# Scheduling priority for the product evacuations of the first FFN group, with 4 raw and 7 operand buffers

## The chip, the cores and the metric

The kernel runs on one core of a Trainium2 chip. The metric is the device time of one execution in microseconds (us). A core has a matrix engine (PE in the profile; PEld is its weight load), a vector engine (DVE), a scalar engine (ACT), a GpSimd engine (POOL) and a queue engine (SP) that only issues transfers. Each works through its own list of instructions strictly in order; semaphores tie the lists together.

## The reference, cut to what matters

One decoder layer is applied to a prompt of 16 + 2048 tokens and to a sample group of 8 x 4 tokens, with the same weights: a mixer (three kinds of heads side by side, then an output product with `w_out`), and a SwiGLU FFN. The change touches the seam between the two and the FFN.

```
y = concat([ya, yb, yc]) @ w_out                 # (tokens, 1024) x (1024, 1024)
h = h + y
g, u = split(rmsnorm(h, norm_ffn) @ w_ffn_in)    # 1024 -> 2 x 2816
h = h + (silu(g) * u) @ w_ffn_out                # 2816 -> 1024
return rmsnorm(h, norm_final), states
```

All inputs are fp32. The kernel keeps fp32 quality by splitting each operand into a high and a low fp16 part and adding three products: high x high, high x low, low x high.

## The kernel before, in words

The kernel is one function, `trunk`, written in the Tile framework. The programmer writes operations and takes tiles from pools with a fixed number of buffers; a scheduler then fixes the order of each engine's list when the kernel is built. It takes the operation of best priority among those that are ready in its model; without further notice priority is the order of the text, and an operation that needs a buffer has to come behind the last reader of that buffer's previous content. Operations that are written under `tc.high_priority()` go ahead of the others that are ready.

**The seam.** After the mixer, `out_early` (L1071) walks over the pairs of 128-token tiles. For each tile it loads the mixer's output from HBM (`xT<-yT_scratch`, L978, SP), multiplies it by `w_out` on PE (48 matmuls of 512 columns for each tile, all at L212, product `wo`), adds the residual on DVE (L998) and stores `h`. The tile of the sample group and the 16 meta tokens (`y`, `xn`, L978 to L992) goes second to last. For the first pairs it also norms the rows and forms the FFN's moving operand (`prep`), stored on ACT's queue as `x_scratch<-pT` (L1043). `load_x2` (L1059) brings that operand of one group back with twelve transposing transfers `x<-x_scratch` (L1057, `DMA_TRANSPOSE`, SP). `interleave` (L874) writes several generators out in turn, one step of each at a time: first `outs`, which is `out_early`, is written out to its end, then `load_x2` of the first group.

**The FFN.** Tokens are worked in three groups of tiles: tiles 1 to 6, 7 to 12, and the rest with the short tile. Within a group the 11 pairs of hidden blocks come in four parts of 2, 3, 3 and 3, and each part is `hidden` for each of its pairs, then `down` for the part. Products of 2 x 2 blocks are made by a seven-product (Winograd) scheme. `quad` (L1230) makes one such product: 7 times 12 matmuls into a PSUM bank `s` (L1239), whose evacuation spreads over ACT, DVE and POOL (L1244 to L1252; POOL has two additions, L1248 and L1249). `hidden` (L1255) makes two quads, one for the gate and one for the up projection, with SiLU on ACT (L1259), the multiplication on DVE (L1262) and the seven operands of the next product as `hh`, high on ACT (L1268) and low on DVE (L1269). `down` (L1285) multiplies `hh` by the weights of `w_ffn_out` (L1292, product `dn`) and adds into the residual `xr` (L1302 to L1330).

**Weight preparation.** Only the first group prepares weights. `gu_operands` (L1179) and `dn_operands` (L1192) load an fp32 block `raw` (SP, L1186 and L1198) and form one operand tile `w`: four additions `sums` on POOL (`left`, L1015 to L1018, for the gate and up weights; `right`, L1022 to L1025, for the down weights), three high parts on ACT (L155) and three low parts on DVE (L156). There are four such tiles for each pair of hidden blocks from the gate and up weights, and two from the down weights, 66 in all. `kept` (L1128) stores each tile to HBM for the later groups, which load it again. The eight loads of the first four `raw` blocks, for the first pair of hidden blocks, are written ahead of the out products (`gu_first`). `raw` has 6 buffers and `w` has 6.

## Time and profile before

| what | value |
|---|---|
| time, median of 3 runs | 2420.63 us (2420.12 to 2420.94) |
| the profiled execution's own time | 2414.44 us |
| its span in the profile | 2412.7 us |
| PE busy | 2220.3 us (92%) |
| DVE busy | 1679.2 us (70%) |
| POOL busy | 1211.7 us (50%) |
| ACT busy | 943.5 us (39%) |
| mean granted clock of TensorE | 0.97 |

The shares are means over stages that differ. By the first matmul of `quad` the mixer and the out products take 1055 us, the first FFN group runs from there to 1602 us, the second from 1602 to about 2015 us with its last `down` running on beside it, and the third to the end. The profiled execution is 6.2 us shorter than the median of the timed runs, so a difference in the profile is to be added to the median, not the profile's end.

### The profile page before, as it was taken

How to read it: one execution, taken by the hardware profiler on the slowest of the kernel's cores; microseconds unless marked ns; L12 is line 12 of the kernel's file. 1: busy time of each engine (PE TensorE's matmuls, PEld its weight loads, DVE VectorE, ACT ScalarE, POOL GpSimd, SP SyncE). 2: the span in 40 equal slices, each digit the busy share in tenths (PEclk: the TensorE clock that was granted, in tenths of full speed). 3: DMA queues.
4: the chain of work that ended last, by engine and by line, in shares of the span. 5: the costliest groups of instructions: out<-in, count | busy, mean ns of one | idle time of the engine just before them, and what ended most of it. 6: DMA issues, size and time to landing. Idle time of an engine off the chain costs nothing. (4 is left out here: it accounts for less than half of the span.)

```text
span 2412.7 us, 51978 instructions
## 1 busy us (share of the span) xinstructions
PE 2220.3 (92%) x20298; PEld 1607.4 (67%) x20298; DVE 1679.2 (70%) x4030; ACT 943.5 (39%) x2526; POOL 1211.7 (50%) x1629
## 2 busy tenths in 40 slices
PE   6989999999999899896989979889999999999996
PEld 6677767767776445444657556567686767888886
DVE  8788988988988756558879677746454535655546
ACT  7554455554554432334343434422212123332323
POOL 7344344444443464549778788744232324544435
PEclk9999999999999899997999989899999999999998
DMA  7232333333223755996436545684324247744441
GB/s 258 50 63 69 66 67 68 75 61 74 66 64 73 173 183 192 275 330 222 153 139 231 196 158 191 191 287 185 148 108 168 108 152 199 269 176 175 177 174 38
DMA packets 294329, 364.95 MB, mean 151 GB/s; under 512 B 203808, under 2 KB 234480, under 8 KB 294067
## 3 DMA queue, kind: packets, MB, share of 16 engines
q1 hardware_dynamic: 285090, 331.02, 43.6%
q0 software_dynamic: 4384, 15.93, 1.7%
q10 hardware_dynamic: 4608, 14.68, 1.7%
q8 instruction: 159, 2.61, 0.4%
q14 instruction: 88, 0.71, 0.1%
HBM read 212.24 MB, written 103.50 MB: 131 GB/s over the span
## 5 line engine op out<-in xcount | busy, mean ns | idle before, releaser
L1239 PE MATMUL s<-x,w 128*128 128x384 f16 (+1 forms) x5544 | 826.4, 312 | 14.8 <-DMA w<-wgu_scratch 6.2
L1239 PEld LDWEIGHTS <-w 128*128 128x128 f16 x5544 | 542.6, 98 | 296.5 <-issue 13.8
L1292 PE MATMUL dn<-w,hh 128*128 128x256 f16 (+1 forms) x4158 | 444.4, 278 | 56.0 <-ACT hh L1268 23.6
L1292 PEld LDWEIGHTS <-hh 128*128 128x128 f16 (+1 forms) x4158 | 379.6, 99 | 119.8 <-ACT hh L1268 27.8
L212 PEld LDWEIGHTS <-xT 128*128 128x128 f16 (+1 forms) x1992 | 177.4, 99 | 191.4 <-issue 25.2
L1268 ACT ACTIVATE hh<-tmp 128x384 f16<-128x384 f32 (+1 forms) x231 | 112.4, 494 | 280.4 <-DVE tmp L1262 164.5
L1248 POOL TENSOR_TENSOR tmp<-tmp,tmp 128x384 f32<-128x384 f32 (+1 forms) x66 | 65.3, 990 | 279.0 <-ACT tmp L1247 271.8
L1269 DVE TENSOR_TENSOR hh<-tmp,hh 128x384 f16<-128x384 f32 (+1 forms) x231 | 144.5, 633 | 74.2 <-ACT hh L1268 72.5
L212 PE MATMUL wo<-wo,xT 128*128 128x512 f16 x768 | 180.8, 394 | 9.5 <-DVE xn L992 4.6
L156 DVE SCALAR_TENSOR_TENSOR w<-raw,w 128x512 f16<-128x512 f32 (+1 forms) x136 | 111.9, 855 | 7.0 <-ACT w L155 6.9
L1250 DVE TENSOR_TENSOR tmp<-s,tmp 128x384 f32<-128x384 f32 (+1 forms) x66 | 34.2, 518 | 107.3 <-PE s L1239 107.3
L212 PE MATMUL d<-xT,qf 128*128 128x128 f16 (+1 forms) x1632 | 107.7, 220 | 0.0
L156 DVE SCALAR_TENSOR_TENSOR w<-sums,w 128x1024 f16<-128x1024 f32 x68 | 96.9, 1427 | 11.4 <-ACT w L155 11.4
L1259 ACT ACTIVATE tmp<-tmp 128x384 f32<-128x384 f32 (+1 forms) x132 | 61.6, 489 | 107.9 <-DVE tmp L1250 52.6
L212 PE MATMUL d<-xT,bqk 128*128 128x128 f16 (+1 forms) x1632 | 100.6, 221 | 3.2 <-DVE e L278 3.2
L1324 DVE SCALAR_TENSOR_TENSOR xr<-dn,xr 128x256 f32<-128x256 f32 x192 | 78.7, 417 | 34.4 <-PE dn L1292 30.2
L212 PEld LDWEIGHTS <-qf 128*128 128x128 f16 x1632 | 94.4, 100 | 9.1 <-issue 4.1
L212 PEld LDWEIGHTS <-bqk 128*128 128x128 f16 x1632 | 94.0, 100 | 5.4 <-issue 4.5
L212 PE MATMUL d<-xT,cq 128*128 128x128 f16 (+1 forms) x1632 | 96.2, 217 | 0.0
L212 PE MATMUL d<-bvo,xT 128*128 128x512 f16 (+1 forms) x408 | 96.2, 380 | 0.0
L1262 DVE SCALAR_TENSOR_TENSOR tmp<-tmp,tmp 128x384 f32<-128x384 f32 (+1 forms) x132 | 71.9, 558 | 34.1 <-POOL tmp L1249 32.6
L212 PE MATMUL d<-aig,xT 128*128 128x512 f16 (+1 forms) x408 | 92.4, 379 | 3.4 <-DVE g L358 3.4
(536 smaller groups left out, 4064.6 us busy)
## 6 DMA issues: line engine op xcount, KB each, us to landing
w<-wgu_scratch SPq DMA_DIRECT2D x88, 896.0 KB
wgu_scratch<-w SPq DMA_DIRECT2D x44, 896.0 KB
w<-wdn_scratch SPq DMA_DIRECT2D x44, 896.0 KB
raw<-in_w_ffn_in_dram SPq DMA_DIRECT2D x88, 256.0 KB
wdn_scratch<-w SPq DMA_DIRECT2D x22, 896.0 KB
xs<-in_x_prompt_dram SPq DMA_DIRECT2D x26, 512.0 KB
x_scratch<-pT ACTq DMA_DIRECT2D x28, 448.0 KB
raw<-in_w_ffn_out_dram SPq DMA_DIRECT2D x22, 512.0 KB
```

What stands on the lines that cost most here:

```text
L156: V.scalar_tensor_tensor(lo, src, scale, hi, op0=ALU.mult, op1=ALU.subtract)
L212: T.matmul(out, lh(k, a), rh(k, b), start=(n == 0), stop=(n == 3 * nk - 1))
L1239: T.matmul(out, A[k // 2][p][:, a, k % 2 * P : k % 2 * P + P], x2[r][:, k // 2, op, k % 2, :n], start=i == 0, stop=i == 11)
L1248: G.tensor_tensor(r12, r12, r22, op=ALU.add)
L1250: V.tensor_tensor(r11, prod(A12, B21), r11, op=ALU.add)
L1259: S.activation(d, d, AF.Silu, scale=UF)
L1262: V.scalar_tensor_tensor(d, v, UF * HS, d, op0=ALU.mult, op1=ALU.mult)
L1268: S.activation(hi, v, AF.Copy)
L1269: V.tensor_tensor(lo, v, hi, op=ALU.subtract)
L1292: T.matmul(out, hh[p][:, q, a, off : off + L], ws[q][r][:, b], start=(q, p, r) == order[0], stop=(q, p, r) == order[-1])
L1324: V.scalar_tensor_tensor(x[:L, cc], m, UD, x[:L, cc], op0=ALU.mult, op1=ALU.add)
```

## The change

Three things change. Every vector, scalar and GpSimd instruction of `quad`, `hidden` and `down` is written under `tc.high_priority()`, through a small wrapper `Ahead` (one line of it, L68 in the changed kernel, then stands as the line of all these instructions). The pool gives `raw` 4 buffers instead of 6 and `w` 7 instead of 6 (the test in `kept` follows). And the out products and the loading of the first group's moving operand, until now written one after the other, are written out in turn by one `interleave`.

```diff
+class Ahead:
+    def __init__(self, tc, engine):
+        self.tc, self.engine = tc, engine
+
+    def __getattr__(self, name):
+        def op(*a, **k):
+            with self.tc.high_priority():
+                return getattr(self.engine, name)(*a, **k)
+        return op
...
     V, S, G, T = nc.vector, nc.scalar, nc.gpsimd, nc.tensor
+    VA, SA, GA = (Ahead(tc, e) for e in (V, S, G))
...
-    w_bufs = [6]
+    w_bufs = [7]
...
-        return pg[0].tile([P, 4, 256], F32, tag="raw", bufs=6, name=nm("raw"))
+        return pg[0].tile([P, 4, 256], F32, tag="raw", bufs=4, name=nm("raw"))
...
-        if w_bufs[0] == 6:
+        if w_bufs[0] == 7:
...
-    interleave(outs)
-    interleave(load_x2(groups[0]))
+    interleave(outs, load_x2(groups[0]))
...
-            S.activation(r11, prod(A11, B11), AF.Copy)
-            V.tensor_tensor(r12, prod(S2, T2), r11, op=ALU.add)
+            SA.activation(r11, prod(A11, B11), AF.Copy)
+            VA.tensor_tensor(r12, prod(S2, T2), r11, op=ALU.add)
...
-            G.tensor_tensor(r12, r12, r22, op=ALU.add)
+            GA.tensor_tensor(r12, r12, r22, op=ALU.add)
```

The same replacement is made in all of `quad`, `hidden` and `down`. No instruction is added or removed on any engine.

**SP at the seam.** These are the rows of SP's list just behind the eight `raw` loads for the first pair of hidden blocks; the names `xT_...` are the mixer's output (two to a token tile), `x_2032` and `x_2033` the high and low part of the first group's moving operand, `w_15778` and its like the operand tiles of the first pair. Before:

```order
L978 DMA xT_2106_16323<-yT_scratch 128x1024
L978 DMA xT_2107_16324<-yT_scratch 128x1024
L1057 DMA_TRANSPOSE x_2032_15773<-x_scratch 128x14x128
L1134 DMA wgu_scratch<-w_15778 128x3584
L1057 DMA_TRANSPOSE x_2033_15774<-x_scratch 128x14x128
L1134 DMA wgu_scratch<-w_15794 128x3584
L978 DMA xT_2128_16637<-yT_scratch 128x1024
L978 DMA xT_2129_16638<-yT_scratch 128x1024
```

Now:

```order
L1072 DMA_TRANSPOSE x_2032_15773<-x_scratch 128x14x128
L1072 DMA_TRANSPOSE x_2033_15774<-x_scratch 128x14x128 x2
L1149 DMA wgu_scratch<-w_15778 128x3584
L1149 DMA wgu_scratch<-w_15794 128x3584
L1072 DMA_TRANSPOSE x_2032_15773<-x_scratch 128x14x128 x2
L1149 DMA wgu_scratch<-w_15810 128x3584
L1149 DMA wgu_scratch<-w_15826 128x3584
L1072 DMA_TRANSPOSE x_2033_15774<-x_scratch 128x14x128 x2
L1072 DMA_TRANSPOSE x_2032_15773<-x_scratch 128x14x128 x2
L1072 DMA_TRANSPOSE x_2033_15774<-x_scratch 128x14x128 x2
L993 DMA xT_2106_16335<-yT_scratch 128x1024
L993 DMA xT_2107_16336<-yT_scratch 128x1024
```

The two loads of the third-last full tile's out product stood first and now stand behind all eleven transposes and four stores. Behind them the list goes on with the two later out products' loads and, between these, the eight `raw` loads of the second pair of hidden blocks, which stood behind everything before.

**DVE at the first evacuation.** These are the rows of DVE's list behind the last residual addition of the out products; `s_16811` is the second product of the first quad, `w_17027` and its like are operand tiles of the second pair. Before:

```order
L998 SCALAR_TENSOR_TENSOR xs_16636<-wo_16726,xs_16636 128x512
L156 SCALAR_TENSOR_TENSOR w_17027<-raw_17028,w_17027 128x512
L156 SCALAR_TENSOR_TENSOR w_17027<-raw_17028,w_17027 128x256
L156 SCALAR_TENSOR_TENSOR w_17043<-raw_17044,w_17043 128x512
L156 SCALAR_TENSOR_TENSOR w_17043<-raw_17044,w_17043 128x256
L1245 TENSOR_TENSOR tmp_16794<-s_16811,tmp_16793 128x384
L1246 TENSOR_TENSOR tmp_16795<-s_16825,tmp_16794 128x384
L156 SCALAR_TENSOR_TENSOR w_17027<-sums_17031,w_17027 128x1024
L156 SCALAR_TENSOR_TENSOR w_17043<-sums_17047,w_17043 128x1024
L1250 TENSOR_TENSOR tmp_16793<-s_16855,tmp_16793 128x384
L156 SCALAR_TENSOR_TENSOR w_17167<-raw_17168,w_17167 128x512
```

Now:

```order
L1013 SCALAR_TENSOR_TENSOR xs_16648<-wo_16738,xs_16648 128x512
L68 TENSOR_TENSOR tmp_16794<-s_16811,tmp_16793 128x384
L68 TENSOR_TENSOR tmp_16795<-s_16825,tmp_16794 128x384
L68 TENSOR_TENSOR tmp_16793<-s_16855,tmp_16793 128x384
L68 TENSOR_TENSOR tmp_16795<-s_16869,tmp_16795 128x384
L1054 SCALAR_TENSOR_TENSOR raw_17331<-raw_17331,ss_17334,gfB_16776 128x1024
L171 SCALAR_TENSOR_TENSOR w_17183<-raw_17184,w_17183 128x512
L68 TENSOR_TENSOR tmp_16794<-s_16883,tmp_16794 128x384
```

The tiles `w_17027`, `w_17043` and `w_17167` now stand ahead of the last residual addition, among the out products. On POOL the sixteen additions of that pair's four tiles move likewise.

**POOL at the last change from `hidden` to `down`.** These are the last sums of the first group, `sums_22127` and `sums_22142`, and the two POOL additions of its last quad, `tmp_21657` and `tmp_21659`, with those of the quad before, `tmp_21519`. Before:

```order
L1249 TENSOR_TENSOR tmp_21519<-tmp_21519,tmp_21518 128x384
L1022 TENSOR_TENSOR sums_22127<-raw_22125 128x256
L1024 TENSOR_TENSOR sums_22127<-raw_22125 128x256
L1023 TENSOR_TENSOR sums_22127<-raw_22125,sums_22127 128x256
L1022 TENSOR_TENSOR sums_22142<-raw_22140 128x256
L1024 TENSOR_TENSOR sums_22142<-raw_22140 128x256
L1025 TENSOR_TENSOR sums_22127<-raw_22125,sums_22127 128x256
L1023 TENSOR_TENSOR sums_22142<-raw_22140,sums_22142 128x256
L1025 TENSOR_TENSOR sums_22142<-raw_22140,sums_22142 128x256
L1248 TENSOR_TENSOR tmp_21657<-tmp_21657,tmp_21659 128x384
L1249 TENSOR_TENSOR tmp_21659<-tmp_21659,tmp_21658 128x384
```

Now:

```order
L68 TENSOR_TENSOR tmp_21519<-tmp_21519,tmp_21518 128x384
L1037 TENSOR_TENSOR sums_22142<-raw_22140 128x256
L1039 TENSOR_TENSOR sums_22142<-raw_22140 128x256
L1038 TENSOR_TENSOR sums_22142<-raw_22140,sums_22142 128x256
L1040 TENSOR_TENSOR sums_22142<-raw_22140,sums_22142 128x256
L68 TENSOR_TENSOR tmp_21657<-tmp_21657,tmp_21659 128x384
L68 TENSOR_TENSOR tmp_21659<-tmp_21659,tmp_21658 128x384
```

One tile's sums have moved further up; the other's still stand ahead of the last quad's two additions. In the second and third group the lists are as they were.

## Rows read from the trace of the kernel before

**Rows 1.** Busy time by stretch: seam, part 1 of group 1 in two.
```profile
core 0: us, PE busy (x) PEld busy (x) DVE busy (x) ACT busy (x) POOL busy (x), PEclk, DMA share, GB/s
997.00:1055.20 58.20, 42.63 (x345) 21.40 (x343) 24.47 (x29) 13.08 (x19) 25.75 (x33) 0.82 1.00 274
1055.20:1109.00 53.80, 53.30 (x327) 31.89 (x326) 41.86 (x49) 24.81 (x45) 42.79 (x47) 1.00 0.83 313
1109.00:1167.30 58.30, 37.39 (x265) 27.41 (x263) 53.86 (x81) 22.77 (x45) 53.54 (x54) 0.77 0.55 199
```
**Rows 2.** PE in order of time: start, length (us), operation, idle before and its releaser.
```profile
984.81 22.61 PE L212 MATMUL wo<-wo,xT 128*128 128x512 f16 x104
1007.26 5.01 PE L212 MATMUL wo<-yT,wo 128*128 128x48 f16 x192
1023.22 1.90 PE L991 MATMUL wo<-ident,y 128*48 128x128 f32 x8 [10.95 <-ACT y L986]
1024.92 7.36 PE L212 MATMUL wo<-wo,xT 128*128 128x512 f16 x24
1036.89 18.52 PE L212 MATMUL wo<-wo,xT 128*128 128x512 f16 x72 [4.61 <-DVE xn L992]
1055.25 1.30 PE L1239 MATMUL s<-x,w 128*128 128x384 f16 x7
```
**Rows 3.** SP's queue, and one row of ACT, in order of time.
```profile
983.45 5.50 SPq L1186 DMA_DIRECT2D raw<-in_w_ffn_in_dram  x8
989.05 0.89 SPq L978 DMA_DIRECT2D xT<-yT_scratch  x2
...
999.32 0.32 SPq L1134 DMA_DIRECT2D wgu_scratch<-w  x1
...
1044.11 9.24 SPq L1057 DMA_TRANSPOSE x<-x_scratch  x3
1053.40 4.66 SPq L1186 DMA_DIRECT2D raw<-in_w_ffn_in_dram  x8
...
1058.45 0.94 ACT L155 ACTIVATE w<-raw 128x512 f16<-128x512 f32 x2 [17.56 <-DMA raw<-in_w_ffn_in_dram]
...
1545.31 19.84 SPq L1057 DMA_TRANSPOSE x<-x_scratch  x9
```
**Rows 4.** The transposes at the seam: least/median/most ns, first and last start.
```profile
L1057 SPq DMA_TRANSPOSE x<-x_scratch x12: 1482/3719/6272, 977.1 to 1051.7; - x12
```
**Rows 5.** Weight preparation in group 1 by form: busy us, mean ns | idle before, releaser.
```profile
L156 DVE SCALAR_TENSOR_TENSOR w<-sums,w 128x1024 f16<-128x1024 f32 x64 | 91.0, 1423 | 8.0 <-ACT w L155 8.0
L156 DVE SCALAR_TENSOR_TENSOR w<-raw,w 128x512 f16<-128x512 f32 x64 | 61.8, 966 | 6.9 <-ACT w L155 6.9
L156 DVE SCALAR_TENSOR_TENSOR w<-raw,w 128x256 f16<-128x256 f32 x64 | 46.3, 724 | 0.0
L1015 POOL TENSOR_TENSOR sums<-raw 128x256 f32<-128x256 f32 x40 | 47.1, 1178 | 43.5 <-DVE w L156 43.4
L1016 POOL TENSOR_TENSOR sums<-sums,raw 128x256 f32<-128x256 f32 x40 | 40.3, 1009 | 0.1
L1017 POOL TENSOR_TENSOR sums<-raw 128x256 f32<-128x256 f32 x40 | 35.2, 881 | 7.7 <-DMA raw<-in_w_ffn_in_dram 7.7
L1018 POOL TENSOR_TENSOR sums<-raw,sums 128x256 f32<-128x256 f32 x40 | 34.8, 870 | 0.9
```
**Rows 6.** Down products by form, group 1 (1055 to 1602).
```profile
L1292 PE MATMUL dn<-w,hh 128*128 128x256 f16 x1386 | 174.4, 289 | 55.0 <-ACT hh L1268 23.6 <-DVE hh L1269 11.7 <-ACT tmp L1302 5.0
```
**Rows 7.** The same in group 2 (1602 to 2015).
```profile
L1292 PE MATMUL dn<-w,hh 128*128 128x256 f16 x1009 | 111.2, 273 | 0.3 <-DVE hh L1269 0.2
```
**Rows 8.** Start of the last down of group 1, in order of time.
```profile
1550.32 0.99 POOL L1249 TENSOR_TENSOR tmp<-tmp,tmp 128x384 f32<-128x384 f32 x1
1551.35 0.56 DVE L1262 SCALAR_TENSOR_TENSOR tmp<-tmp,tmp 128x384 f32<-128x384 f32 x1 [4.12 <-POOL tmp L1249]
1552.43 43.48 PE L1292 MATMUL dn<-w,hh 128*128 128x256 f16 x367 [3.55 <-DVE hh L1269]
```
**Rows 9.** The moving operand's stores, among the page's DMA issues (KB each).
```profile
x_scratch<-pT ACTq DMA_DIRECT2D x28, 448.0 KB
```

More of the change, by code (lines that the diff above doesn't have):

```diff
@@ L1243, in quad @@
             r11, r12, r21, r22 = (tmp()[:, :n] for _ in range(4))
-            S.activation(r11, prod(A11, B11), AF.Copy)
-            V.tensor_tensor(r12, prod(S2, T2), r11, op=ALU.add)
-            V.tensor_tensor(r21, prod(S3, T3), r12, op=ALU.add)
-            S.activation(r22, prod(S1, T1), AF.Copy)
-            G.tensor_tensor(r12, r12, r22, op=ALU.add)
-            G.tensor_tensor(r22, r22, r21, op=ALU.add)
-            V.tensor_tensor(r11, prod(A12, B21), r11, op=ALU.add)
-            V.tensor_tensor(r21, prod(A22, T4), r21, op=ALU.add)
-            V.tensor_tensor(r12, prod(S4, B22), r12, op=ALU.add)
+            SA.activation(r11, prod(A11, B11), AF.Copy)
+            VA.tensor_tensor(r12, prod(S2, T2), r11, op=ALU.add)
+            VA.tensor_tensor(r21, prod(S3, T3), r12, op=ALU.add)
+            SA.activation(r22, prod(S1, T1), AF.Copy)
+            GA.tensor_tensor(r12, r12, r22, op=ALU.add)
+            GA.tensor_tensor(r22, r22, r21, op=ALU.add)
+            VA.tensor_tensor(r11, prod(A12, B21), r11, op=ALU.add)
+            VA.tensor_tensor(r21, prod(A22, T4), r21, op=ALU.add)
+            VA.tensor_tensor(r12, prod(S4, B22), r12, op=ALU.add)
             return r11, r12, r21, r22
@@ L1258, in hidden @@
             for d in sg:
-                S.activation(d, d, AF.Silu, scale=UF)
+                SA.activation(d, d, AF.Silu, scale=UF)
             up = quad(gu_first.pop(0) if gu_first else gu_operands(DFF + 2 * jq * P), n)
             for d, v in zip(sg, up):
-                V.scalar_tensor_tensor(d, v, UF * HS, d, op0=ALU.mult, op1=ALU.mult)
+                VA.scalar_tensor_tensor(d, v, UF * HS, d, op0=ALU.mult, op1=ALU.mult)
             a11, a21, a12, a22 = sg
@@ L1267, in put @@
                 hi, lo = (hh[a][:, q, op, :n] for a in range(2))
[L1268 to L1269 removed]
+                SA.activation(hi, v, AF.Copy)
+                VA.tensor_tensor(lo, v, hi, op=ALU.subtract)
             put(A11, a11)
@@ L1273, in hidden @@
             put(A22, a22)
-            G.tensor_tensor(s1, a21, a22, op=ALU.add)
+            GA.tensor_tensor(s1, a21, a22, op=ALU.add)
             put(S1, s1)
-            G.tensor_tensor(s2, s1, a11, op=ALU.subtract)
+            GA.tensor_tensor(s2, s1, a11, op=ALU.subtract)
             put(S2, s2)
-            G.tensor_tensor(s3, a11, a21, op=ALU.subtract)
+            GA.tensor_tensor(s3, a11, a21, op=ALU.subtract)
             put(S3, s3)
-            G.tensor_tensor(s4, a12, s2, op=ALU.subtract)
+            GA.tensor_tensor(s4, a12, s2, op=ALU.subtract)
             put(S4, s4)
@@ L1301, in down @@
                 m1, m5, u2, u3 = (tmp()[:, :256] for _ in range(4))
-                S.activation(m1, prod(0), AF.Copy, scale=UD)
-                V.scalar_tensor_tensor(u2, prod(1), UD, m1, op0=ALU.mult, op1=ALU.add)
-                V.scalar_tensor_tensor(u3, prod(2), UD, u2, op0=ALU.mult, op1=ALU.add)
-                S.activation(m5, prod(3), AF.Copy, scale=UD)
+                SA.activation(m1, prod(0), AF.Copy, scale=UD)
+                VA.scalar_tensor_tensor(u2, prod(1), UD, m1, op0=ALU.mult, op1=ALU.add)
+                VA.scalar_tensor_tensor(u3, prod(2), UD, u2, op0=ALU.mult, op1=ALU.add)
+                SA.activation(m5, prod(3), AF.Copy, scale=UD)
                 parts = [prod(i) for i in (4, 5, 6)]
@@ L1317, in down @@
                         parts.append(tmp()[:L, :256])
-                        S.activation(parts[-1], out, AF.Copy, scale=UD if i0 == 0 else 1.0)
+                        SA.activation(parts[-1], out, AF.Copy, scale=UD if i0 == 0 else 1.0)
                 m1, u2, u3, m5 = parts[:4]
                 parts = parts[4:]
-                G.tensor_tensor(u2, u2, m1, op=ALU.add)
-                G.tensor_tensor(u3, u3, u2, op=ALU.add)
+                GA.tensor_tensor(u2, u2, m1, op=ALU.add)
+                GA.tensor_tensor(u3, u3, u2, op=ALU.add)
             for x, cc, m in ((x1, c1, parts[0]), (x2_, c1, parts[1]), (x1, c2, parts[2])):
-                V.scalar_tensor_tensor(x[:L, cc], m, UD, x[:L, cc], op0=ALU.mult, op1=ALU.add)
-            V.tensor_tensor(x1[:L, c1], x1[:L, c1], m1, op=ALU.add)
-            G.tensor_tensor(u2, u2, m5, op=ALU.add)
-            V.tensor_tensor(x1[:L, c2], x1[:L, c2], u2, op=ALU.add)
-            V.tensor_tensor(x2_[:L, c1], x2_[:L, c1], u3, op=ALU.add)
-            G.tensor_tensor(u3, u3, m5, op=ALU.add)
-            G.tensor_tensor(x2_[:L, c2], x2_[:L, c2], u3, op=ALU.add)
+                VA.scalar_tensor_tensor(x[:L, cc], m, UD, x[:L, cc], op0=ALU.mult, op1=ALU.add)
+            VA.tensor_tensor(x1[:L, c1], x1[:L, c1], m1, op=ALU.add)
+            GA.tensor_tensor(u2, u2, m5, op=ALU.add)
+            VA.tensor_tensor(x1[:L, c2], x1[:L, c2], u2, op=ALU.add)
+            VA.tensor_tensor(x2_[:L, c1], x2_[:L, c1], u3, op=ALU.add)
+            GA.tensor_tensor(u3, u3, m5, op=ALU.add)
+            GA.tensor_tensor(x2_[:L, c2], x2_[:L, c2], u3, op=ALU.add)
         def prep_late(pr):
```

2 lines of the change are left out of this document (removed).

## The prediction

> **What bounds the kernel now.** I read the busy shares first: PE is busy 92% of the span, so a time can only move where PE waits or runs at a lower clock. The stretches show where that is [rows 1]. In the seam, 997 to 1055 us, PE is busy 42.6 of 58.2 us; in the second half of part 1, where `down` runs, 37.4 of 58.3 us, while DVE is busy 53.9 and POOL 53.5: there the weight preparation on DVE and POOL is the bound. Between the two PE is busy 53.3 of 53.8 us. The groups of instructions say the same of the whole first FFN group: in `down` PE waited 55.0 us, 23.6 of them for `hh` from ACT and 11.7 for `hh` from DVE [rows 6], and in group 2, where no weights are prepared, 0.3 us [rows 7]. So preparation costs some tens of us of PE, and the seam some 20. Groups 2 and 3 have nothing that the change touches.
>
> **Part 1: the loads at the seam.** This edit stands in the code but is no matter of priority: with `interleave(outs, load_x2)` SP's list has eleven transposes and four operand stores ahead of the two `xT` loads of the third-last full tile, which stood directly behind the eight `raw` loads. The transposes were spread over 977 to 1052 us before, with the `xT` loads in between [rows 4]. A transposing transfer holds SP's queue: three in a row took 9.24 us, 3.08 each [rows 3]; nine in a row at the end of the group took 19.84, 2.20 each [rows 3]; the median of the twelve at the seam is 3.72 [rows 4]. I take 3.0, the nearest row being the run of three in the same busy stretch, and keep 2.2 and 3.72 as ends. The count starts where the `raw` loads end, 983.45 + 5.50 = 989.0 [rows 3]. Eleven transposes are 33 us; four stores at about half a us are 2 (0.32 is one [rows 3]); the first store waits for its operand, as it did until 999.32, which is 4.3 us if three transposes stand ahead of it. The `xT` loads then issue at 989.0 + 33 + 2 + 4.3 = 1028.3. From issue to use takes 5.05 us, as the first `raw` row issued at 1053.40 and was read by ACT at 1058.45 [rows 3]. So PE can start the product at about 1033 (with 2.2 a transpose 1025, with 3.72 1041).
>
> PE needs it much earlier. The stretch of 104 matmuls from 984.81 [rows 2] ends with the 48 of this tile, at 22.61/104 = 0.217 us each, so the product began at 984.81 + 22.61 - 48 x 0.217 = 997. PE therefore stands about 36 us (28 to 44) where it stood none. Nothing covers this: PE's list has no other work ahead of the first quad.
>
> What remains for PE from there is 48 x 0.217 = 10.4 (this tile), 5.01 and 1.90 (the short tile), and 96 x 0.217 = 20.9 (the last two tiles) [rows 2]: 38.2 us. Before, PE needed 1055.25 - 997 = 58.2 for it, with 20 us of waits and of slow clock: 10.95 for `y`, 4.61 for `xn` [rows 2], the granted clock 0.82 on the mean [rows 1]. Part of these goes away because other work proceeds while PE stands, the transposes among it. I leave 7 us of waits, 2 for `y` on ACT, which now has more weight preparation ahead of it, and 5 for the last pair, whose residual load stands behind an operand store and the loads of the second pair's `raw`. I add 3 for a clock that is low after the long gap: behind the wait of 10.95 the 24 matmuls took 7.36/24 = 0.307 each instead of 0.217 [rows 2], 4.3 us for 48 of them. The first quad then starts at 1033 + 38.2 + 7 + 3 = 1081, against 1055.25: **+26 us**. Least: 1025 + 38.2 + 1 = 1064, +9. Most: 1041 + 38.2 + 17 = 1096, +41, with before's waits kept nearly in full.
>
> The Trainium skill ("DMA: Bandwidth & Descriptors", Latency and other measured facts) gives a transposing transfer 261 GB/s with a non-contiguous middle dimension. A store of this operand is 448 KB [rows 9], so the run of nine moved 459 KB in 2.20 us, 208 GB/s, and the trace doesn't reach the figure; by it one would take an estimated 1.76 us, eleven 19.4 instead of 33, and the time would be about 2421, that of the first rival below.
>
> **Part 2: preparation that moves ahead.** The eight `raw` loads of the second pair stood behind all of the seam, at 1053.40 [rows 3], and now stand between the last out products' loads. Their four tiles' POOL sums, and on DVE three of four tiles, run while PE is in the seam. POOL is busy only 25.8 of 58.2 us there [rows 1], and the seam grows, so there is room. One tile costs POOL 1.178 + 1.009 + 0.881 + 0.870 = 3.94 us and DVE 1.423 + 0.966 + 0.724 = 3.11 [rows 5]. Four tiles leave POOL's list of part 1: 15.8 us. Against this the seventh buffer lets preparation run one tile further ahead, so one tile of the next part is pulled into part 1: 3.9 back. POOL is relieved of 12 us in part 1. DVE had begun two of the tiles ahead of the first evacuation already; it is relieved of two sums' low parts and one whole tile, 2 x 1.42 + 3.11 = 6.0, and with the tile pulled in of 2.9. Both engines are bound in that stretch [rows 1], and PE's wait follows whichever is later. I take **-12**, POOL's figure, because a sum comes ahead of the high and low parts that DVE makes from it; the ends are 6 (DVE) and 17 (all four tiles and a little clock back).
>
> The Trainium skill ("SBUF — State Buffer", Who interferes with whom) has a DVE instruction with two SBUF inputs and a GpSimd instruction contend for a shared port pair that is locked. Here the low parts of 256 columns have a mean of 724 ns [rows 5]. By that rule the busy times add up, and the relief would be 12 + 2.9 = 15, a total of about 2432.
>
> **Part 3: buffers and priority.** With six buffers the POOL sums waited 43.4 us for DVE's last read of a `w` tile and 7.7 for `raw` [rows 5]; fewer `raw` buffers move the second figure, which at most doubles, 7.7 more on an engine that waits for DVE anyway. I price this at nothing, the end at +8. At the group's end one tile more is done early; PE is busy there for 43.48 us without a break [rows 8], so it gains nothing. The priority moves no instruction past weight preparation in the two places where it should matter: at the last change to `down`, four sums still stand ahead of the last quad's two POOL additions, and that is where DVE waited 4.12 and PE 3.55 us [rows 8]. One tile's sums fewer ahead is an effect of the seventh buffer. Priced at nothing, with the rival below.
>
> **The sum.** 2414.44 + 26 - 12 = 2428.4 on the profiled execution's scale; the median is 6.2 above it, so 2420.63 + 14 = **2435 us**. The ends of the forecast are narrower than the bounds, which don't meet all at once: a first quad 19 us later with a relief of 14 gives 2426, one 37 later with a relief of 12 gives 2446.
>
> **The rivals.**
> *No net change.* The transposes run at 2.2 each, as in the run of nine [rows 3], or faster, and the waits at the seam vanish in PE's gap: the first quad comes 12 us later, relief 12: 2421. For it: the long ones in [rows 4] share the engines with other loads. Against it: the DMA share in that stretch is 1.00 [rows 1].
> *More loss.* The waits at the seam stay in full, +41, and the relief is DVE's 6 only: 2456. For it: ACT and DVE have more preparation ahead of the short tile and the last residuals.
> *Faster: the priority works.* If PE's waits for `hh` in `down` come from evacuations standing behind weight preparation, and the new order cures that over all four parts, it is worth up to 23.6 + 11.7 = 35.3 us [rows 6]: 2435 - 35 = 2400 in full, 2417 with half. It decides from 14 us on, the net loss of the other parts. Against it: the order on POOL at the last change to `down` has hardly moved, and in part 1 DVE and POOL are full [rows 1], so that order alone can't help. For it: DVE's list at the first evacuation has lost its weight preparation.
>
> **How the numbers follow.** Chances: forecast 0.55, no change 0.18, more loss 0.12, faster 0.15. A difference of 0.2%, 4.8 us, is about what a measurement of this kernel can tell from none. Faster 0.15 (the last rival), same 0.18 (the first), slower 0.55 + 0.12 = 0.67. The range reaches from 2411, which takes in about the nearer half of the faster rival and all of no change, to 2452, about half of more loss. That leaves out 0.07 below and 0.07 above.
>
> **What would show it.** In the profile of the changed kernel: SP's transposes in one run from 989 to about 1025; a gap of PE of 28 to 44 us from 997 on; the first quad at about 1081 (1064 to 1096); a granted clock in that stretch under 0.82; the first FFN group from its first quad to its end about 535 instead of 547 us; PE's wait for ACT's `hh` about 15 instead of 23.6 us; groups 2 and 3 unchanged in length. The prediction is wrong if PE doesn't stand at 997, if the first quad is before 1064, or if the first group shortens by more than 17 us; the last would be the priority's work.

## The result, and the profile after

The changed kernel takes 2440.04 us (median of 5 runs, 2433.05 to 2446.16) against 2420.63 (median of 5, 2416.97 to 2422.91): a ratio of 1.0077, 95% interval 1.0053 to 1.0102, 19.4 us slower. The profiled execution took 2441.3 us with a span of 2439.6, 26.9 us more than the profiled span of before.

Where do the 26.9 us come from? Four landmarks divide both spans: the end of the sample group's last mixer matmul on PE (978.61 before, 983.54 after), the first quad (1055.25, 1088.65), the first quad of group 2 (1602.09, 1629.07) and the end. I call the stretch between the first two the seam.

| stretch | before | after | difference |
|---|---|---|---|
| mixer, to the start of the seam | 978.61 | 983.54 | +4.9 |
| seam | 76.64 | 105.11 | +28.5 |
| group 1 | 546.84 | 540.42 | -6.4 |
| groups 2 and 3 | 810.6 | 810.5 | -0.1 |

The first line is not put down to the change. Up to the seam the lists of all five engines hold the same operations in the same order in both kernels, and in the profiles of the other kernels below, all but one of which (`loads_first`) share PE's list up to there, the seam begins between 978.0 and 986.3 us. The change is worth 28.5 - 6.4 = 22 us in the profiles.

SP's queue at the seam, in order of time (start, length, operation), answers to [rows 3]:

```profile
988.63 5.79 SPq L1201 DMA_DIRECT2D raw<-in_w_ffn_in_dram  x8
994.47 9.20 SPq L1072 DMA_TRANSPOSE x<-x_scratch  x3
1005.83 2.00 SPq L1149 DMA_DIRECT2D wgu_scratch<-w  x2
1007.89 6.31 SPq L1072 DMA_TRANSPOSE x<-x_scratch  x2
1018.78 4.00 SPq L1149 DMA_DIRECT2D wgu_scratch<-w  x2
1022.83 15.64 SPq L1072 DMA_TRANSPOSE x<-x_scratch  x6
1038.57 1.00 SPq L993 DMA_DIRECT2D xT<-yT_scratch  x2
```

Eleven transposes take 9.20 + 6.31 + 15.64 = 31.15 us, 2.83 each, and only behind them do the `xT` loads issue, 44 us after the first transpose. On PE (columns as in [rows 2]) the wait is there in one piece:

```profile
983.48 18.52 PE L227 MATMUL wo<-wo,xT 128*128 128x512 f16 x85
1042.27 1.89 PE L227 MATMUL wo<-wo,xT 128*128 128x512 f16 x4 [40.27 <-DMA xT<-yT_scratch]
1064.11 1.90 PE L1006 MATMUL wo<-ident,y 128*48 128x128 f32 x8 [4.61 <-ACT y L1001]
1065.80 23.01 PE L227 MATMUL wo<-wo,xT 128*128 128x512 f16 x96
1088.65 54.76 PE L1253 MATMUL s<-x,w 128*128 128x384 f16 x336
```

So the seam's 28.5 us add up: 40.27 of a new wait, less 10.95 of the other waits (15.56 in two of them before [rows 2], 4.61 in one now), less 0.9 of busy PE. By stretch (columns as in [rows 1]; seam from the gap's start, `hidden` of part 1, `down` of part 1):

```profile
1002.00:1088.65 86.65, 41.77 (x344) 21.48 (x345) 34.21 (x38) 19.17 (x28) 40.03 (x49) 0.72 0.82 249
1088.65:1143.20 54.55, 54.55 (x337) 32.87 (x336) 38.05 (x49) 25.41 (x48) 34.49 (x37) 1.00 0.60 219
1143.20:1198.80 55.60, 36.64 (x254) 26.67 (x252) 49.70 (x77) 18.51 (x36) 50.59 (x53) 0.75 0.57 209
```

`hidden` and `down` of part 1 in the kernel before, cut at the same landmarks, the first matmul of `quad` and the first `dn` matmul:

```profile
1055.25:1111.84 56.59, 55.09 (x337) 32.77 (x336) 44.70 (x52) 26.99 (x49) 45.63 (x49) 1.00 0.81 302
1111.84:1167.28 55.44, 35.54 (x253) 26.51 (x254) 51.00 (x77) 20.56 (x42) 50.68 (x52) 0.75 0.56 204
```

The preparation did move: POOL is busy 40.0 us in the seam instead of 25.8 [rows 1], and 34.5 instead of 45.6 in `hidden` of part 1. But `hidden` was bound by PE before and is now (54.55 of 54.55), and `down` of part 1, where I had expected the gain, is as long as it was, 55.6 us against 55.4, with POOL as busy as it was, 50.6 against 50.7. Group 1's 6.4 us come from elsewhere, mostly from its last part (139.3 instead of 146.0 us). The start of the last `down`, which answers to [rows 8]:

```profile
1581.86 1.04 PE L1306 MATMUL dn<-w,hh 128*128 128x256 f16 x4 [6.13 <-ACT hh L68]
1583.22 41.70 PE L1306 MATMUL dn<-w,hh 128*128 128x256 f16 x367 [0.32 <-DVE hh L68]
1629.07 11.12 PE L1253 MATMUL s<-x,w 128*128 128x384 f16 x57 [4.15 <-DMA w<-wgu_scratch]
```

The wait of 3.55 us is 0.32, the 367 matmuls take 41.70 instead of 43.48, and the wait ahead of group 2 is 4.15 instead of the 6.18 of before:

```profile
1602.09 56.60 PE L1239 MATMUL s<-x,w 128*128 128x384 f16 x336 [6.18 <-DMA w<-wgu_scratch]
```

Over the whole group PE's waits in `down` fell from 55.0 [rows 6] to 49.5 us, and those for ACT's `hh` only from 23.6 to 22.1:

```profile
L1253 PE MATMUL s<-x,w 128*128 128x384 f16 x1848 | 303.1, 326 | 10.9 <-DVE tmp L68 10.0 <-ACT tmp L68 0.6 <-DVE xr L68 0.3
L1306 PE MATMUL dn<-w,hh 128*128 128x256 f16 x1386 | 173.0, 287 | 49.5 <-ACT hh L68 22.1 <-DVE tmp L68 9.2 <-DVE hh L68 5.5
```

### The profile page after: what moved, and what is told of

The parts are those of the page before. It is cut to its first block, busy times and chain, and to the rows that moved or that the text cites. A ratio compares the mean times of both kernels' runs of the same rounds, so it can differ in the third digit from the quotient of the medians.

```text
span 2439.6 us, 51935 instructions
## 1 busy us (share of the span) xinstructions
PE 2221.8 (91%) x20298; PEld 1607.2 (66%) x20298; DVE 1680.3 (69%) x4030; ACT 944.3 (39%) x2526; POOL 1203.1 (49%) x1629
## 5 line engine op out<-in xcount | busy, mean ns | idle before, releaser
L68 POOL TENSOR_TENSOR tmp<-tmp,tmp 128x384 f32<-128x384 f32 (+3 forms) x424 | 395.2, 939 | 529.7 <-ACT tmp L68 325.6
L1306 PE MATMUL dn<-w,hh 128*128 128x256 f16 (+1 forms) x4158 | 443.0, 277 | 50.4 <-ACT hh L68 22.1
L1306 PEld LDWEIGHTS <-hh 128*128 128x128 f16 (+1 forms) x4158 | 378.3, 99 | 114.0 <-issue 26.9
L68 DVE TENSOR_TENSOR tmp<-s,tmp 128x384 f32<-128x384 f32 (+1 forms) x330 | 169.6, 517 | 304.1 <-PE s L1253 277.2
L68 ACT ACTIVATE hh<-tmp 128x384 f16<-128x384 f32 (+1 forms) x231 | 112.2, 493 | 263.6 <-DVE tmp L68 149.1
L68 DVE TENSOR_TENSOR hh<-tmp,hh 128x384 f16<-128x384 f32 (+1 forms) x231 | 144.7, 633 | 74.1 <-ACT hh L68 72.4
L68 ACT ACTIVATE tmp<-dn 128x256 f32<-128x256 f32 (+1 forms) x184 | 68.1, 377 | 196.7 <-PE dn L1306 178.6
L68 ACT ACTIVATE tmp<-s 128x384 f32<-128x384 f32 (+1 forms) x132 | 59.4, 455 | 218.9 <-PE s L1253 218.7
L68 DVE TENSOR_TENSOR xr<-xr,tmp 128x256 f32<-128x256 f32 (+1 forms) x216 | 126.1, 595 | 6.9 <-POOL tmp L68 1.6
L68 ACT ACTIVATE tmp<-tmp 128x384 f32<-128x384 f32 (+1 forms) x132 | 61.5, 490 | 113.1 <-DVE tmp L68 98.7
L68 DVE SCALAR_TENSOR_TENSOR xr<-dn,xr 128x256 f32<-128x256 f32 x192 | 78.9, 416 | 34.6 <-PE dn L1306 30.3
L170 ACT ACTIVATE w<-sums 128x1024 f16<-128x1024 f32 x68 | 71.3, 1048 | 72.9 <-POOL sums L1033 58.1
```

The costliest lines, as they stand in the source:

```text
L68: return getattr(self.engine, name)(*a, **k)
L170: S.activation(hi, src, AF.Copy, scale=scale)
L1306: T.matmul(out, hh[p][:, q, a, off : off + L], ws[q][r][:, b], start=(q, p, r) == order[0], stop=(q, p, r) == order[-1])
```

## The experiments

All the kernels' stretches, worked out from the starts of PE's rows in their profiles. "Down 1" is the part of part 1 from the first `dn` matmul to the first quad of part 2; the ratio is to the kernel before, timed beside it on the same chip.

| kernel | seam | part 1 (down 1) | part 2 | part 3 | part 4 | seam + group 1 | ratio (95%) |
|---|---|---|---|---|---|---|---|
| before | 76.6 | 112.0 (55.4) | 142.0 | 146.8 | 146.0 | 623.5 | |
| changed | 105.1 | 110.2 (55.6) | 140.6 | 150.3 | 139.3 | 645.5 | 1.0077 (1.0053 to 1.0102) |
| turns_only | 104.8 | 109.3 (54.5) | 143.7 | 144.8 | 145.9 | 648.5 | 1.0091 (1.0067 to 1.0115) |
| no_turns | 70.5 | 118.2 (59.3) | 140.9 | 149.9 | 139.8 | 619.3 | 0.9993 (0.9974 to 1.0013) |
| act_queue | 121.8 | 111.6 (57.0) | 140.7 | 150.4 | 139.4 | 663.8 | 1.0140 (1.0111 to 1.0168) |
| five_ahead | 104.5 | 111.0 (56.4) | 140.7 | 150.4 | 139.4 | 646.0 | 1.0075 (1.0048 to 1.0102) |
| loads_first | 72.3 | 119.9 (59.8) | 141.3 | 150.4 | 140.5 | 624.3 | 1.0014 (1.0000 to 1.0029) |
| load_late | 74.0 | 118.5 (59.1) | 141.3 | 150.3 | 140.9 | 625.0 | 1.0001 (0.9983 to 1.0019) |
| prep_early | 87.2 | 116.7 (54.3) | 140.5 | 150.0 | 139.8 | 634.2 | 1.0052 (1.0032 to 1.0072) |
| raw4 | 75.3 | 108.3 (52.8) | 147.7 | 144.1 | 145.8 | 621.2 | 0.9990 (0.9971 to 1.0009) |
| sums_pair2 | 78.5 | 112.7 (56.8) | 141.9 | 147.0 | 146.3 | 626.5 | one run |
| sums_pair3 | 73.8 | 115.0 (53.1) | 143.2 | 143.7 | 145.7 | 621.4 | one run |
| dve_pair2 | 71.0 | 112.1 (52.5) | 142.1 | 146.9 | 146.5 | 618.6 | one run |
| dve_pair3 | 71.9 | 107.9 (50.4) | 141.9 | 146.8 | 146.0 | 614.5 | one run |

A part repeats far better than a whole run: part 2, which several of these kernels leave alone, is 141.9 to 142.1 in four of them, while whole runs of the kernel before spread over 2410.4 to 2435.4 us. The seam repeats less well: the eight kernels whose SP issues at the seam in the order of before (before, `no_turns`, `load_late`, `raw4` and the last four) have 70.5 to 78.5. Where a kernel's first quad comes early, it waits up to 4.2 us for the last transpose, so seam and part 1 are to be read together.

### Which of the three edits

The first two kernels take the edits apart. `turns_only` is the kernel before with the one line of the generators:

```diff
-    interleave(outs)
-    interleave(load_x2(groups[0]))
+    interleave(outs, load_x2(groups[0]))
```

> The kernel before with one edit: the out products and the loading of the first group's moving operand are written out in turn; 6 raw and 6 operand buffers, no priority. Theory (the transposes ahead of the xT loads on SP cost the time): PE stands about 40 us ahead of the third-last full tile's out product, the first quad starts about 28 us later against the seam's start, and the eight raw loads of the second pair stand early as in the changed kernel; 2440 to 2450 us, the upper half if the seventh operand buffer brought the 6 us that the first group gained. Rival (the loss comes from 4 raw buffers or from the priority): no gap on PE, about 2421.

It took 2445.97 against 2423.32 us. PE's gap is there without the other edits:

```profile
1040.29 1.89 PE L212 MATMUL wo<-wo,xT 128*128 128x512 f16 x4 [36.92 <-DMA xT<-yT_scratch]
...
1088.02 42.25 PE L1238 MATMUL s<-x,w 128*128 128x384 f16 x259
```

`no_turns` is the reverse, the changed kernel with the two calls of `interleave` apart again.

> The changed kernel with that one edit taken back: the two generators are written out one after the other, priority and 4 raw and 7 operand buffers stay. Theory: no gap on PE at the seam; the last down of group 1 starts with a wait of about 0.3 instead of 3.55 us because one tile's sums fewer stand ahead of the last quad's additions, and the second group's entry wait shrinks by some 2: 2414 to 2419 us, 1 to 7 under the kernel before. Rival (buffers or priority cost the time): 2430 to 2440.

2421.62 against 2423.32 us, and the seam is 70.5 us. So the line of the turns makes the loss, and only it; the rival is refuted. The gain of 1 to 7 us that I expected is not shown: 1.7 us lie inside the interval, and the time is above the 2414 to 2419 that I gave. The last `down` of `no_turns` starts as in the changed kernel:

```profile
1557.60 41.74 PE L1307 MATMUL dn<-w,hh 128*128 128x256 f16 x367 [0.33 <-DVE hh L68]
```

while `turns_only` starts it as before the change (3.57 us of wait, 43.46 of work), so the 6 us of part 4 come from the buffers. What remains is the priority. It has no run of its own; the lists show it: the kernel before with the wrappers alone has the same operations in the same order on PE, DVE, POOL and SP, and on ACT one pair of neighbours, 25 rows ahead of its end, stands the other way round. And `no_turns` differs from a kernel with the buffers alone by that same pair, the changed kernel from one with the buffers and the turns as well. In the title's first half the change does nothing.

### Why the turns cost time

`act_queue` moves the transposing loads of the first group off SP:

```diff
-        nc.sync.dma_start(x2[a][:, q, :, :, off : off + P].rearrange("p o k n -> p (o k) n"), src, transpose=True)
+        eng = nc.scalar if off_sp[0] else nc.sync
+        eng.dma_start(x2[a][:, q, :, :, off : off + P].rearrange("p o k n -> p (o k) n"), src, transpose=True)
```

> The changed kernel with the first group's transposing loads issued on ACT's queue instead of SP's. Theory (SP's order alone makes the gap): the xT loads issue right behind the raw loads, PE's gap of 40 us at the third-last full tile is gone; the wait for y of the short tile stays or grows to some 20 us, since ACT is held by the transposes, about 3 us each; 2405 to 2425 us. Rival (the transposes crowd the DMA engines whatever queue issues them, so that xT lands late): a gap of 20 us or more stays at that place, 2432 or more.

The gap at the third-last full tile is gone, so it was SP's order that made it. (Only the first of the eleven transposes had been issued there when `xT` was loaded, so this run doesn't try whether eleven in flight would make `xT` late; in the changed kernel PE starts 3.7 us after `xT` issues behind all of them.) Yet the kernel is the slowest of all, 2457.67 us, where I expected 2405 to 2425: the wait for `y` of the short tile, which I had expected at some 20 us, took the gap's place and is longer. PE, and ACT's queue and ACT, in order of time:

```profile
1000.96 10.53 PE L227 MATMUL wo<-wo,xT 128*128 128x512 f16 x48 [1.06 <-DMA xT<-yT_scratch]
1011.33 5.01 PE L227 MATMUL wo<-yT,wo 128*128 128x48 f16 x192
1067.58 1.90 PE L1006 MATMUL wo<-ident,y 128*48 128x128 f32 x8 [51.24 <-ACT y L1001]
```

```profile
1018.24 36.75 ACTq L1075 DMA_TRANSPOSE x<-x_scratch  x8
1055.09 1.06 ACT L210 ACTIVATE y<-pb 128x1024 f16<-128x1024 f32 x1 [39.55 <-issue]
```

Eight transposes in a row took 36.75 us on ACT's queue, in which ACT did nothing else. Their mean of 4.6 us says little, since one of them took half of the time (least/median/most ns):

```profile
L1075 ACTq DMA_TRANSPOSE x<-x_scratch x8: 1657/2214/17666, 1018.2 to 1052.7; - x8
```

Why that one took 17.67 us is not shown. On both engines the engine that issues a transposing load stood while it was issued, and what was queued behind it paid.

`five_ahead` begins the loading twelve steps later, so that five transposes and two stores stand ahead of `xT`:

```diff
-    interleave(outs, load_x2(groups[0]))
+    interleave(outs, late(load_x2(groups[0]), 12))
```

(`late` yields twelve times and then passes the generator on.)

> The changed kernel with the moving operand's loading begun twelve steps of the out products later: five transposes and two stores stand ahead of the xT loads instead of eleven and four, and the raw loads of the second pair come behind nearly all of the seam again. Theory (each transpose holds SP for about 2.9 us): xT issues some 20 us earlier than in the changed kernel, PE's gap is 15 to 20 instead of 40 us; the first quad some 8 to 12 us later than before; 2420 to 2430 us. Rival (a gap that doesn't go by the number of transposes): 35 us or more, 2435 or more, or none at all, 2416.

A miss, and the most useful one. PE's gap shrank from 40.3 to 26.3 us, more than the 15 to 20 that I expected to be left (the second stores wait for their operands until 1020), but the seam is as long as in the changed kernel, 104.5 us, and the time is too, 2440.46 us. PE waits later instead:

```profile
1026.38 1.89 PE L227 MATMUL wo<-wo,xT 128*128 128x512 f16 x4 [26.29 <-DMA xT<-yT_scratch]
...
1051.03 1.90 PE L1006 MATMUL wo<-ident,y 128*48 128x128 f32 x8 [6.58 <-ACT y L1001]
1052.72 17.28 PE L227 MATMUL wo<-wo,xT 128*128 128x512 f16 x72
1078.86 7.47 PE L227 MATMUL wo<-wo,xT 128*128 128x512 f16 x24 [8.86 <-DVE xs L1013]
```

The wait of 8.86 us is for the residuals of the last pair. Their buffers come free when the pair before is prepared (`pT`), and on DVE that preparation now stands among the operand tiles (`w`) of the second pair, whose `raw` loads issue from 1041.8 us on instead of 1053.4, ahead of it; SP's loads of the residuals (`xs`) stand behind three operand stores that wait as well. DVE, then SP:

```profile
1062.39 4.02 DVE L171 SCALAR_TENSOR_TENSOR w<-sums,w 128x1024 f16<-128x1024 f32 x1 [0.84 <-ACT w L170]
1066.33 1.21 DVE L171 SCALAR_TENSOR_TENSOR pT<-pb,pT 128x1024 f16<-128x1024 f32 x1
1070.61 1.33 DVE L171 SCALAR_TENSOR_TENSOR w<-sums,w 128x1024 f16<-128x1024 f32 x1 [3.07 <-ACT w L170]
1071.87 2.07 DVE L171 SCALAR_TENSOR_TENSOR pT<-xs,pT 128x512 f16<-128x512 f32 x2
```

```profile
1058.71 13.58 SPq L1149 DMA_DIRECT2D wgu_scratch<-w  x3
1074.55 1.14 SPq L115 DMA_DIRECT2D xs<-in_x_prompt_dram  x2
```

So a second suspect stood beside the transposes: the second pair's preparation inside the seam, which my prediction had booked only as a gain.

`loads_first` keeps the turns and writes the out products' loads under high priority.

```diff
-        load_x(x, t)
-        if t == 0:
+        with tc.high_priority():
+            load_x(x, t)
+            if t == 0:
```

> The changed kernel with the loads of the out products (the mixer's output and the residual) written under high priority; the generators still take turns. SP's list then has the xT loads of the last tiles ahead of ten of the transposes and the second pair's raw loads behind everything again. Theory (the place of the xT loads among the transposes is what cost the time): no gap of PE at the third-last full tile, the first quad at most 5 us later than before, 2412 to 2424 us. Rival (the turns cost in another way, through the preparation that they pull forward or the DMA engines): 2432 or more.

2424.58 against 2422.77 us, seam 72.3. Its seam isn't quite like the others': 27 of the out products' matmuls, some 6 us, have moved ahead of its start. `load_late` is `five_ahead` with 24 steps instead of 12.

> The changed kernel with the moving operand's loading begun 24 steps of the out products later, so that all xT loads stand ahead of all but a few transposes, and the second pair's raw loads behind everything. It differs from the changed kernel without turns by the last xT loads, which stand some four transposes earlier. Theory (PE there waits for y and xn behind the transposes, not for the last xT): the same within 5 us, 2415 to 2425. Rival (the last tiles' xT is late in the kernel before): 5 to 10 us less than before, 2411 to 2416.

2422.46 against 2422.77 us, seam 74.0. My expectation had its lists wrong: with 24 steps they hold the same operations in the same order as those of `no_turns`, on all five engines, so this is a second profile of that kernel and says nothing on the rival. Both kernels are without the loss, and in both the `xT` loads of the third-last full tile stand ahead of all eleven transposes; but both also have the second pair's preparation behind the seam again. They don't tell the two suspects apart. `prep_early` does: `no_turns` with the second pair's operands written ahead of the out products.

```diff
-    gu_first = [gu_operands(c) for c in (0, DFF)]
+    gu_first = [gu_operands(c) for c in (0, DFF, 256, DFF + 256)]
```

> The changed kernel without the turns, and with the second pair's gate and up tiles written ahead of the out products like the first pair's. SP's list then has the xT loads of the third-last full tile ahead of all but one transpose, as before the change, and the second pair's raw loads and stores among the out products, earlier even than in the changed kernel. In all kernels so far with a seam of 104 to 105 us (from the end of the sample group's last mixer matmul to the first quad; 70 to 79 in the others) both came together, transposes ahead of xT and the second pair's preparation inside the seam, and the kernel with five transposes ahead lost at the end of the seam what it won at its start. Theory (the transposes ahead of xT): seam 75 to 88 us, time 2412 to 2428. Rival (the second pair's preparation inside the seam, on ACT and DVE ahead of the last tiles' residuals and on the DMA engines): seam 95 to 110, time 2435 or more.

2432.70 against 2419.56 us, with a seam of 87.2 us (5 of them a wait between the last out product and the first quad) and a wait of 4 more right behind the first quad's start. The seam is where the theory put it, at the upper end; the time is above its range and below the rival's. PE has no gap for `xT` and waits 13.14 us for `xn`, whose load stands on SP behind three operand stores:

```profile
984.05 29.00 PE L227 MATMUL wo<-wo,xT 128*128 128x512 f16 x133
1028.11 1.90 PE L1006 MATMUL wo<-ident,y 128*48 128x128 f32 x8 [10.20 <-ACT y L1001]
1049.19 17.13 PE L227 MATMUL wo<-wo,xT 128*128 128x512 f16 x72 [13.14 <-DVE xn L1007]
1078.10 52.20 PE L1254 MATMUL s<-x,w 128*128 128x384 f16 x306 [4.05 <-DMA x<-x_scratch]
```

```profile
1031.00 9.92 SPq L1149 DMA_DIRECT2D wgu_scratch<-w  x3
1041.01 0.38 SPq L112 DMA_DIRECT2D xn<-in_x_sample_dram  x1
```

Preparation that stands this early therefore costs by itself: seam and group together take 15.0 us more than in `no_turns` (634.2 against 619.3), from which this kernel differs by that edit alone, and 10.8 more than before, with one transpose ahead of the `xT` loads, as before the change. In the changed kernel, where it stands later and seam and group take 22.0 us more than before, it can have made little of that: beside the 40.27 us for `xT`, PE's only wait in the seam is the 4.61 for `y`. What it would make without the gap shows in `five_ahead`, where with a part of the gap taken away the residuals are late next. A kernel with the transposes ahead of `xT` and the preparation behind the seam wasn't run.

### Why the preparation that moved gave so little

My prediction took 12 us off part 1 because POOL and DVE lost that much work there. `sums_pair2` and `sums_pair3` take POOL's additions of four tiles away, once for tiles prepared during `hidden` of part 1 and once for tiles prepared during its `down`; the edit in `gu_operands` (256 is the second pair, 512 the third):

```diff
+            if c0 % DFF == 256:
+                operands(w, raw[:, :, 0:P], a[1][1], raw, WG)
+                return
             left(w, sum_tile(), a[0][0], a[0][1], a[1][0], a[1][1], raw[:, :, 0:P], WG)
```

> The kernel before, with the POOL additions of the second pair's four gate and up operand tiles left out (the raw block stands in their place, so those weights are wrong); ACT's and DVE's work on them stays. It takes 16 additions, 15.8 us by the trace of before, off POOL in the stretch where hidden of part 1 runs. Theory (there PE is the bound, so work taken away there gives PE nothing): part 1, from the first quad to the first quad of part 2, shortens from 112.0 by at most 4 us. Rival (POOL's work counts in part 1 wherever it stands, as my prediction had it): shorter by 10 to 16 us.

Part 1 is 112.7 us, its `down` 56.8: nothing gained, as the theory had it.

> The same for the third pair's four tiles, which are prepared while down of part 1 runs. Theory (there POOL and DVE are the bound): part 1 shortens by more than in the kernel without the second pair's additions, 5 to 14 us of its 112.0, as POOL is relieved of 15.8 and DVE of nothing. Rival (DVE alone is the bound of that stretch, busy 53.9 of 58.3 us): at most 3.

Part 1 is 115.0, 4.2 of which are a wait for the last transpose, since the seam was short; its `down` is 53.1 instead of 55.4. Taking 15.8 us off POOL in the very stretch that POOL filled gave at most 2.3 us, and perhaps nothing: seam and part 1 together are 188.8 against 188.7, and the preparation ran on during the wait of 4.2. The row of `down` shows POOL relieved and DVE not:

```profile
1107.00:1167.50 60.50, 42.33 (x299) 31.16 (x298) 53.67 (x87) 24.25 (x49) 43.29 (x45) 0.77 0.55 192
```

My expectation of 5 to 14 us was wrong; so the next two take the same tiles off DVE:

```diff
         S.activation(hi, src, AF.Copy, scale=scale)
+        if on_act[0]:
+            S.activation(lo, src, AF.Copy, scale=scale)
+            return
         V.scalar_tensor_tensor(lo, src, scale, hi, op0=ALU.mult, op1=ALU.subtract)
```

> The kernel before, with the low parts of the second pair's four gate and up tiles made by ACT as a plain copy instead of DVE's subtraction (so those weights are wrong): 4 x 3.11 = 12.4 us off DVE in the stretch of hidden of part 1, some 8 more on ACT. Theory (PE is the bound in that stretch): part 1 stays within 3 us of 112.0. Rival (DVE's total over part 1 sets its end): 8 to 12 us shorter.

> The same for the third pair's four tiles, prepared while down of part 1 runs. Theory, after the run without POOL's additions there gave PE nothing with DVE still busy 53.7 us of the stretch: DVE alone is the bound, and part 1 shortens by 5 to 12 of its 112.0 us. Rival (the stretch hangs on the chain from the last quad's additions over hh, not on an engine's load): at most 2 us.

With 12.4 us off DVE, part 1 stays at 112.1 us for the second pair (3.5 of them a wait for the last transpose), and is 107.9 for the third: `down` 52.5 and 50.4 instead of 55.4. The 52.5, with nothing taken off the stretch of `down` itself, shows how little 2.3 us mean there. DVE's load seems to count for more than POOL's, but only 5.0 of 12.4 us come back even in the stretch itself. In that run the wait at the entry of `down` is as long as ever, 10.01 us (first row) where the kernel before (second row) has 9.88:

```profile
1128.45 1.89 PE L1299 MATMUL dn<-w,hh 128*128 128x256 f16 x8 [10.01 <-ACT hh L1275]
...
1124.62 1.89 PE L1292 MATMUL dn<-w,hh 128*128 128x256 f16 x8 [9.88 <-ACT hh L1268]
```

Neither theory nor rival describes this well: part of PE's wait in `down` goes by DVE's load, and half of it in the kernel before (9.88 of 19.9 us) stands at the entry, behind the chain that by the code runs from the last quad over POOL's additions to `hh`. That wait moves without `down` following it: it is 6.22 us in `sums_pair2` and 7.27 in the changed kernel, whose `down` is as long as before or longer. What bounds `down` of part 1 stays open.

### The buffers

`raw4` is the kernel before with 4 raw buffers.

```diff
-        return pg[0].tile([P, 4, 256], F32, tag="raw", bufs=6, name=nm("raw"))
+        return pg[0].tile([P, 4, 256], F32, tag="raw", bufs=4, name=nm("raw"))
```

> The kernel before with 4 raw buffers instead of 6 and nothing else. In the kernel with both buffer edits, part 1 took 118.2 us instead of 112.0, part 3 149.9 instead of 146.8 and part 4 139.8 instead of 146.0. Theory (fewer raw buffers cost, the seventh operand buffer gains): part 1 and part 3 are as long as there, 116 to 120 and 149 to 151, part 4 stays at 146; the time 2426 to 2436. Rival (raw buffers are without effect, as the prediction priced them): all parts as in the kernel before, 2418 to 2426.

The theory falls: part 1 is 108.3 us and part 3 144.1, shorter than before, part 2 is 147.7, longer, and the four add up to 545.9 against 546.8; the time is 2420.23 against 2422.71. Fewer raw buffers shift preparation between the parts and cost nothing that this measurement can tell from none. So, comparing `no_turns` with `raw4`, it is the seventh operand buffer, which pulls one tile forward, that lengthens part 1 (118.2, of which 2.3 are a wait for the last transposes, against 108.3) and part 3 (149.9 against 144.1) and shortens parts 2 and 4 (140.9 against 147.7, 139.8 against 145.8). With 7 operand buffers and 5 or 6 raw ones the pool doesn't fit into the memory, so the seventh was tried with 4 raw ones alone. No version here beats the kernel before clear of the interval; `no_turns` and `raw4` are level with it.

## Why the prediction was right, and where it was not

**Sign and size.** 2435 was forecast, 2411 to 2452; 2440.04 was measured. The likeliest case, a loss at the seam and a smaller gain in group 1, is what happened: +28.5 and -6.4 where the sum had +26 and -12. Measured against the seam's own start, the first quad came 2.5 us later than forecast. That the whole came so near is in part luck: the -6.4 is not the gain that I forecast in part 1, which was 1.9, but mostly one of 6.7 in part 4, which I had priced at nothing; and the seam of one and the same order on SP scatters by 8 us between profiles.

**The transposes on SP.** Right in kind and nearly in size. 2.83 us each against 3.0 taken; PE's gap 40.3 against 36 (28 to 44). What made up the difference are the four stores between the transposes. Each is issued in a third of a us, but each waited on SP until DVE had made its low part, 11.1 us in all, where I had counted 2 us of stores and one wait of 4.3 (issues: least/median/most ns; waits: total, times, longest):

```profile
L1149 SPq DMA_DIRECT2D wgu_scratch<-w x4: 319/332/343, 1005.8 to 1022.5; - x4
SPq L1149 <- DVE w L171: 11.1, 4, 4.5
```

The 4.3 was an error of my own too: three transposes of 3.0 from 989.0 end at 998.0, which leaves 1.3 until 999.32, so that the sum should have had a gap of 33. The granted clock of the stretch is 0.72, under the 0.82 of [rows 1]. The sentence that rested on the Trainium skill ("DMA: Bandwidth & Descriptors", Latency and other measured facts) is answered: at its 261 GB/s a transpose would have taken an estimated 1.76 us; the trace has 2.83, and the measurement decides.

**What else the turns do at the seam.** Here the prediction had a hole. It took the early preparation of the second pair as a pure gain that fits into idle time of POOL and DVE, and left 7 us for waits behind it. `prep_early` shows a loss of 15.0 us against `no_turns` from that preparation alone, where it stands still earlier. The sum still came out, because in the changed kernel it cost little: only 4.6 us of waits were left behind the gap. It did not run while PE stood, for its `raw` loads stood behind the transposes as well; POOL idled until they had come:

```profile
1047.19 0.72 POOL L1032 TENSOR_TENSOR sums<-raw 128x256 f32<-128x256 f32 x1 [25.84 <-DMA raw<-in_w_ffn_in_dram]
```

But PE came 40 us late to the last tiles, and the preparation was done when the last pair was due. In `five_ahead`, where PE comes out of its gap at 1026.4 instead of 1042.3 and the `raw` loads issue no sooner, it showed. Of the two sizes, one (the gap) was right, and the other (what lies under it) was never on trial in the forecast.

**The relief of part 1, -12.** This step failed. The row that I quoted [rows 1] has two stretches: PE busy 53.3 of 53.8 us in `hidden`, and DVE and POOL full in `down`. I added up the tiles that leave part 1 and let them shorten `down`; the tiles left `hidden`, where PE is the bound. Cut at the same landmarks, POOL's busy time fell from 45.6 to 34.5 us in `hidden` and stayed in `down`, 50.7 and 50.6. `down` stayed at 55.6 against 55.4 and `hidden` gained 2.0 (56.6 to 54.6). Moreover a busy engine is not yet the bound: 15.8 us off POOL in `down` itself were worth at most 2.3, 12.4 us off DVE 5.0. The sign that I had named, a wait for ACT's `hh` of about 15 us and a first group of about 535, failed with it: 22.1 and 540.4. (My low end of 6 for DVE also left out the tile that is pulled in; by my own count it was 2.9.) By the other rule that I weighed, the Trainium skill's "SBUF — State Buffer" (Who interferes with whom), the relief would have been larger still, 15. In `sums_pair3`, where POOL had less to do in that stretch, DVE's low parts of 256 columns did get shorter, from a mean of 799 to 667 ns, which goes with the rule, but those of the sums did not (1363 and 1452); whether PE gained by it the run doesn't show.

**The seventh buffer at the group's end, 0.** Also wrong, in the other direction: part 4 gains 6.7 us, and 6.0 in `no_turns` against `raw4`. I had quoted the row that shows it [rows 8]: PE waits there for DVE, DVE for POOL's addition, and two tiles' sums stand ahead of that. One tile's sums fewer takes 3.2 us off the chain; I saw the order and priced it at nothing because PE has no break once it has begun. The rest of the gain lies in the matmuls behind (1.8) and in the wait ahead of group 2 (2.0), which I don't explain. In `no_turns` the other parts lose the gain again (part 3 gets 3.1 longer than before), so that the buffers as a whole are worth about nothing there, as the sum had it, but not for its reason; beside the turns group 1 is 3.4 us shorter with them (540.4 against 543.8), which the two ratios don't tell apart. Why part 3 gets longer I didn't settle.

**Raw buffers and priority at nothing.** Both right, the first by `raw4`, the second by the lists. The rival that the priority cures the waits for `hh` had 0.15; 22.1 of its 23.6 us are still there.

## What to carry to other kernels

When two generators are written out in turn, go through each issuing queue and ask what each transfer that moves forward now stands ahead of, and do that for what the scheduler pulls forward in its wake too: here it was the stores of freshly prepared operands, which hold the queue until their operand is ready. Work that moves off an engine shortens a stretch only if it leaves the stretch in which that engine ends last, and even there a run with the work left out tells what it is worth, since a busy share doesn't. A scheduling priority acts only on operations that are ready at the same time; compare the lists before pricing it.

## What the runs showed of the hardware

A transposing load of 448 KB held the engine that issued it: 2.83 us each on SP at the seam in the changed kernel, and on ACT in `act_queue` eight in a row for 36.75 us, while ACT did nothing else. That it holds ACT's own instructions as well as its queue I had expected. Seven of the eight took 1.66 to 3.75 us, about as on SP; the eighth took 17.67, and whether the queue or the other transfers of that stretch made it so long stays open.
